# Hidden and gathered token operands interleaved in one tile, and every expert pass inside the two arms of TensorE's branch

## The chip, the cores and the metric

The kernel runs on one core of one Trainium2 chip. The metric is the device time of that core in microseconds, from launch to end, of the whole program. A core has TensorE for matrix products (PE in the profile, with its loads of the stationary operand listed apart as PEld), VectorE (DVE), ScalarE (ACT), GpSimd (POOL) and SyncE (SP), each with its own instruction queue, and 16 DMA engines. The on-chip memory SBUF has 128 partitions; matmul results go to the eight banks of PSUM.

## What is computed

The reference is a two-layer trunk over 256 tokens of width 1024: layer one is an RWKV-7 time mix and a dense SwiGLU block, layer two a forgetting attention and a mixture of experts, with an RMS norm ahead of each block and at the end. The change touches the mixture of experts:

```python
logits = (xf @ w_router).astype(jnp.float32)
top_v, top_i = lax.top_k(logits, K)            # K = 2 of E = 8 experts
gates = jax.nn.softmax(top_v, axis=-1)
...
def expert_block(args):
    e, tok, wt = args
    return swiglu(xf[tok], w_gu[e], w_down[e]).astype(jnp.float32) * wt[:, None]
```

`swiglu` is `(silu(x @ w_gate) * (x @ w_up)) @ w_down`, with inner width 3584. The 512 choices of 256 tokens spread over eight experts, 64 each on average. Everything is fp32.

## The kernel before, in words

**Precision.** TensorE multiplies in a one-pass fp32 format (`F32R`) that keeps fewer bits. Each operand is therefore split in two, a high part that is its cast (ACT) and a low part that is the rest (DVE): `split`, L213 to L215. A product is the sum of three passes: high weight by high token, low weight by high token, high weight by low token.

**Weights.** `Weights` (L166) streams all weights as tiles of 128x2048 fp32 (1 MB) from two DMA queues in turn, SP and POOL (L180). In the expert stage seven raw buffers are in use (three `wraw`, four `mob`; three more, `hpool`, take a tile once and later hold the hidden activations). Each tile is split to `wh` (four buffers) and `wl` (three buffers), two tiles ahead of their use in program order (`get`, L206). A raw buffer is free for the next DMA when its split is done; a `wh` or `wl` buffer when TensorE has used it.

**Order.** Up to the end of the RWKV block the order is written by hand. From there a scheduler orders the instructions of each engine by priority (their place in the program) and by when its own cost model has them ready, and places all semaphores. What stands inside a `tc.If` is one unit for it: nothing from outside is put between. Each engine then runs its list strictly in order.

**An expert** (`for e in range(E)`, L1639) has 42 weight tiles, 28 for gate and up and 14 for down, worked through in 21 pairs (`pair`, L1505). Gate and up go by chunks of the inner width, three of 1024 and one of 512 (`CH`, L373; `up_chunk`, L1541), down in seven pairs (`down`, L1587). The tokens are the stationary operand, 128 slots wide; the weights stream through, 512 columns per matmul.

**Short and long experts.** An expert with at most 64 tokens (short) leaves half the slots free, and these hold the low parts: slots 0 to 63 are the high parts, slots 64 to 127 the low parts of the same tokens. Two passes then give all three products, and a `fold` matmul (L1538, L1539) adds rows 64 to 127 to rows 0 to 63 of the result. ACT casts the result to `gc`, times a 0/1 factor `mode.short`, for it. The fold is issued for all experts; for one with more than 64 tokens (long) it adds zeros. Only the third pass, `third`, stands in a branch that TensorE alone takes (L1527), on the token count loaded into a register (L1641). A pair does `two(0)` for its first tile, `third` for both tiles in the branch, other work (`hooks[0]`), `two(1)`, `hooks[1]`.

**Around a chunk.** After gate's last pair comes `gc`, and in up's first pair the fold and SiLU (`first_half`). After up come `gc`, fold and product (`second_half`) in the next chunk's first pair, and in its second pair four TensorE transposes per 512 columns and their split into `hx` (`transposes`, L1562 to L1571): two ACT instructions for the two halves of the slots, a DVE subtraction, and a DVE multiply-add that puts the low parts of short experts into slots 64 to 127.

**Gather and scatter.** `gather` (L1463) takes the tokens of two experts at once: DVE builds one-hot matrices `ohs` from the slot positions, matmuls of 256 columns with the normed tokens `muh` and `mul` give `xgh` and `xgl` (48 matmuls in all), and ACT casts them. It also transposes the one-hots to `ohT` for `scatter` (L1596), which adds the gated result to `res`. The first gather stands before expert 0, the others in the down part of experts 1, 3 and 5. A fallback for experts with over 128 tokens (L1660) follows, and isn't entered with these inputs.

**Memory.** `mu32`, the normed tokens that the router reads (L1714), shares its place with `xgh`; `xgl` and `hx` have tiles of their own, `hx` with two high and two low parts one after the other.

## Time and profile before

| | |
|---|---|
| time, median of three runs | 1691.68 us (1690.11 to 1696.17) |
| time of the profiled execution | 1692.88 us |
| its span, first to last instruction | 1691.0 us |
| TensorE matmul busy | 1555.7 us (92%) |
| VectorE busy | 1297.7 us (77%) |
| ScalarE busy | 1106.7 us (65%) |
| DMA traffic | 445.73 MB, mean 264 GB/s |
| expert stage, first matmul to last | 713.1 to 1671.5 us |

The profile is of one execution. Busy times count work on the engine itself; waits, branches and the issue of DMAs aren't busy. In a row of a group, what is written stands left of the arrow and what is read right of it; then come the number of instructions, their busy time together, the mean duration of one in ns, and the engine's idle time just before them with what ended most of it. In a row of the timeline the first number is the start and the second the duration of a run of equal instructions. Matmuls are pipelined: four that take 1.07 us together start 0.23 us apart, though one alone shows 0.39.

### The profile page before, as it was taken

What the parts mean: (1) busy time and instruction counts of PE and PEld (TensorE: products, weight loads), DVE (VectorE), ACT (ScalarE), POOL (GpSimd) and SP (SyncE); (2) the same over time, 40 slices, a digit from 0 to 9 for tenths busy, and PEclk for the clock granted to TensorE, in tenths of its full rate; (3) what the DMA queues carried; (4) which work ended last, traced back from release to release, by engine and by line L of the source; (5) the groups of instructions that cost most, each with busy time, mean ns of one, the idle gap of its engine ahead of it and who ended that gap; (6) DMA issues with size and microseconds to landing.
All of it is one profiled execution on the core that took longest, in us unless ns stands there. A gap on an engine that the chain in (4) does not pass through costs nothing. (4 is left out here: it accounts for less than half of the span.)

```text
span 1691.0 us, 20004 instructions
## 1 busy us (share of the span) xinstructions
PE 1555.7 (92%) x7275; PEld 1201.5 (71%) x7275; DVE 1297.7 (77%) x1357; ACT 1106.7 (65%) x1148; POOL 176.7 (10%) x230
## 2 busy tenths in 40 slices
PE   5998998999999999998889999999988889888996
PEld 4655876888888887766566788788665567566885
DVE  5587557555546556699899888888899899998985
ACT  4633245444435665598688777677788798797783
POOL 0412010000000000011111111110111111111110
PEclk9998598999999999799899999999999999999999
DMA  5233133555555442579899999899899999999982
GB/s 178 88 109 104 22 106 132 189 180 199 183 193 181 150 150 100 224 297 384 347 397 370 364 357 362 327 358 341 312 387 397 360 401 370 382 383 368 373 338 84
DMA packets 156816, 445.73 MB, mean 264 GB/s; under 512 B 24129, under 2 KB 29425, under 8 KB 156705
## 3 DMA queue, kind: packets, MB, share of 16 engines
q1 hardware_dynamic: 105440, 262.95, 42.4%
q0 software_dynamic: 45920, 176.31, 27.5%
q10 hardware_dynamic: 5344, 5.01, 1.0%
q8 instruction: 67, 1.10, 0.3%
q14 instruction: 45, 0.36, 0.1%
HBM read 442.12 MB, written 2.11 MB: 263 GB/s over the span
## 5 line engine op out<-in xcount | busy, mean ns | idle before, releaser
L215 DVE TENSOR_TENSOR wl<-raw,wh 128x2048 fp32r<-128x2048 f32 x398 | 890.6, 2284 | 108.9 <-PE acc L219 35.3
L214 ACT CAST wh<-raw 128x2048 fp32r<-128x2048 f32 x398 | 752.6, 1914 | 304.4 <-PE pgu L220 51.4
L1503 PE MATMUL pgu<-wh,xgh 128*128 128x512 f32 x896 | 259.7, 408 | 10.5 <-ACT wh L214 3.9
L1503 PE MATMUL pgu<-wl,xgh 128*128 128x512 f32 x896 | 252.3, 403 | 13.7 <-DVE wl L215 13.7
L1503 PEld LDWEIGHTS pgu<-wh,xgh 128*128 128x128 f32 x896 | 169.5, 195 | 64.1 <-issue 22.5
L1503 PEld LDWEIGHTS pgu<-wl,xgh 128*128 128x128 f32 x896 | 171.7, 193 | 54.4 <-DVE wl L215 18.0
L1503 PE MATMUL acc<-wh,hx 128*128 128x512 f32 x616 | 165.2, 399 | 5.2
L180 POOL DMA_DIRECT2D raw<-in_moe_w_gu_dram x112 | 79.9, 714 | 668.7 <-DVE wl L215 556.4
L1503 PEld LDWEIGHTS acc<-wh,hx 128*128 128x128 f32 x616 | 113.3, 189 | 41.3 <-issue 12.7
L1503 PE MATMUL acc<-wl,hx 128*128 128x512 f32 x448 | 127.3, 402 | 3.0 <-DVE wl L215 2.1
L1503 PEld LDWEIGHTS acc<-wl,hx 128*128 128x128 f32 x448 | 82.2, 189 | 28.9 <-DVE wl L215 11.5
L218 PE MATMUL pgu<-wh,uh 128*128 128x512 f32 x224 | 89.3, 399 | 1.9 <-ACT wh L214 1.9
L219 PE MATMUL pgu<-wl,uh 128*128 128x512 f32 x224 | 88.2, 394 | 1.6 <-DVE wl L215 1.6
L220 PE MATMUL pgu<-wh,ul 128*128 128x512 f32 x224 | 88.2, 394 | 0.0
L1503 PE MATMUL pgu<-wh,xgl 128*128 128x512 f32 x336 | 85.0, 395 | 0.0
L1503 PE MATMUL pgu<-gc,fold 128*128 128x512 f32 x112 | 50.7, 464 | 37.1 <-ACT gc L1538 35.4
L1503 PEld LDWEIGHTS pgu<-wh,xgl 128*128 128x128 f32 x336 | 63.1, 188 | 14.9
L1538 ACT ACTIVATE gc<-pgu,cnt 128x512 fp32r<-128x512 f32 x112 | 72.3, 692 | 1.3 <-PE pgu L1503 1.3
L180 POOL DMA_DIRECT2D raw<-in_moe_w_down_dram x56 | 39.4, 704 | 294.8 <-DVE wl L215 165.2
L1503 PEld LDWEIGHTS pgu<-gc,fold 128*128 128x128 f32 x112 | 21.1, 189 | 64.0 <-ACT gc L1538 60.3
L1570 DVE TENSOR_TENSOR hx<-pht,hx 128x512 fp32r<-128x512 f32 x56 | 37.3, 689 | 32.2 <-ACT hx L1569 32.2
L219 PEld LDWEIGHTS pgu<-wl,uh 128*128 128x128 f32 x224 | 42.8, 191 | 10.7 <-DVE wl L215 2.0
(366 smaller groups left out, 2185.2 us busy)
## 6 DMA issues: line engine op xcount, KB each, us to landing
raw<-in_moe_w_gu_dram SPq DMA_DIRECT2D x112, 1024.0 KB, 9.6
raw<-in_moe_w_gu_dram POOLq DMA_DIRECT2D x112, 1024.0 KB, 9.7
raw<-in_moe_w_down_dram SPq DMA_DIRECT2D x56, 1024.0 KB, 8.9
raw<-in_moe_w_down_dram POOLq DMA_DIRECT2D x56, 1024.0 KB, 8.6
raw<-in_ffn_w_gu_dram SPq DMA_DIRECT2D x28, 1024.0 KB, 5.4
raw<-in_fox_w_in_dram SPq DMA_DIRECT2D x16, 1024.0 KB, 5.7
raw<-in_ffn_w_down_dram SPq DMA_DIRECT2D x14, 1024.0 KB, 4.9
raw<-in_rwkv_w_rkv_dram SPq DMA_DIRECT2D x24, 512.0 KB, 4.4
```

The source lines that it names most:

```text
L180: (nc.gpsimd if self.nd >= N_EARLY and self.nd % 2 else nc.sync).dma_start(t, src)
L214: nc.scalar.copy(hi, src)
L215: nc.vector.tensor_tensor(lo, src, hi.bitcast(F32), ALU.subtract)
L218: nc.tensor.matmul(o, lh, rh, start=first, stop=False)
L219: nc.tensor.matmul(o, lh, rl, start=False, stop=False)
L220: nc.tensor.matmul(o, ll, rh, start=False, stop=last)
L1503: nc.tensor.matmul(o, l, r, start=first, stop=last, skip_group_check=True)
L1538: nc.scalar.activation(gc, p, AF.Copy, scale=mode.short)
L1570: nc.vector.tensor_tensor(l, p, h.bitcast(F32), ALU.subtract)
```

## The change

- Both parts lie in turns in one tile: `xg` is `[128, KB, 2, 128, 2]` and `hx` `[128, 2, 4, 128, 2]`, the last index being high or low. A long expert reads 128 slots of one part with a step of two elements; a short one reads the first 64 slots of both parts, which lie next to each other, as 128. So nothing has to be placed into slots 64 to 127, and the hidden activations go by a plain `split`, written with a step of two.
- All passes of a pair stand in the branch: `passes(False)` in one arm (three passes per tile), `passes(True)` in the other (two). The fold and the transposes stand in the arms too (`arms`), after the pair's passes; the other work (`todo`) comes after the branch, once per pair.
- The fold is issued in the short arm alone; since high and low rows alternate, it adds odd rows to even ones. The cast to `gc` stays for all, without a factor. In the short arm the transposes are matmuls with `evens`, the identity with its even columns first.
- The gather makes the two parts by two products each; the one-hots for the scatter come from slot numbers (`slots`) halved for short experts by a new constant `half`.
- `mu32` moves to the tiles of `ul` in another pool, and `uh` and `ul` of the expert stage are made after the positions.

```diff
@@ fox
             if step == 12:
+                norm2.u32 = [npool.tile([128, 4, T], F32, name=f"mu32{i}", tag=f"ul{i}") for i in range(2)]
...
@@ gather
+            for i in range(n):
+                nc.vector.scalar_tensor_tensor(slots[:, i, :], cc("half"), shorts[i], cc("iota"), ALU.mult, ALU.add)
             for t in range(2):
-                nc.vector.tensor_scalar(oh2[:, t, 0:n, 0:64], cc("iota", 0, 64)[:, None, :].to_broadcast([128, n, 64]),
-                                        0.0, None, ALU.mult)
                 for i in range(n):
...
+                    nc.vector.tensor_scalar(ohs[:, 0, t, i, :], cc("iota"), pcols[i](t), None, ALU.is_equal)
+                    nc.vector.tensor_scalar(ohs[:, 1, t, i, :], slots[:, i, :], pcols[i](t), None, ALU.is_equal)
+            g = rot.tile([128, KB, 2, 128, 2], F32R, name="xg", bufs=1)
+            for part, src in enumerate((uh, ul)):
                 for k2 in range(4):
...
+                        for t in range(2):
                             nc.tensor.matmul(p[:, j * n * 128:(j + 1) * n * 128], src[t][:, k * 128:(k + 1) * 128],
-                                             o[:, t, 0:n, :], start=(q == 0), stop=(q == len(prods) - 1))
-                    nc.scalar.copy(g[:, k2 * 2:k2 * 2 + 2, 0:n, :],
+                                             ohs[:, 0, t, 0:n, :], start=(t == 0), stop=(t == 1))
+                    nc.scalar.copy(g[:, k2 * 2:k2 * 2 + 2, 0:n, :, part],
                                    p[:, 0:2 * n * 128].rearrange("p (j i t) -> p j i t", j=2, i=n))
...
@@ pair
-            def two(i):
...
-            def third():
...
+            def passes(short):
+                for i in range(2):
+                    for part, at in ((0, 0), (1, 0)) if short else ((0, 0), (0, 1), (1, 0)):
+                        for ti, j, k in blocks:
+                            if ti == i:
+                                l = lhs(k)[:, 0:64, :].rearrange("p s a -> p (s a)") if short else lhs(k)[:, :, at]
+                                for b, o in enumerate(out):
+                                    mm(o, l, ws[i][part][:, j, b * 512:(b + 1) * 512], k == 0 and part == at == 0,
+                                       i == 1 and part == 1)
+                for f in arms:
+                    f(short)
+
+            if many is None:
+                passes(False)
             else:
-                with tc.If(mode.many > 64):
-                    third()
...
+                with tc.If(many > 64) as arm:
+                    passes(False)
+                with arm.Else():
+                    passes(True)
+            for f in todo:
                 f()
...
@@ folded
-            nc.scalar.activation(gc, p, AF.Copy, scale=mode.short)
-            return lambda: mm(p, fold, gc, last=True)
+            nc.scalar.copy(gc, p)
+            return lambda short: short and mm(p, fold, gc, last=True)
...
@@ up_chunk
-            def transposes(b):
...
-                h, l = hidden(n0 // 512 + b)
-                nc.scalar.copy(h[:, :, 0:64], p[:, :, 0:64])
-                nc.scalar.activation(h[:, :, 64:128], p[:, :, 64:128], AF.Copy, scale=mode.other)
-                nc.vector.tensor_tensor(l, p, h.bitcast(F32), ALU.subtract)
-                nc.vector.scalar_tensor_tensor(h[:, :, 64:128], l[:, :, 0:64].bitcast(F32), mode.short,
-                                               h[:, :, 64:128].bitcast(F32), ALU.mult, ALU.add)
+            def transposes(is_short):
+                pht[:] = pht or [ps("pht") for _ in range(nb)]
+                for b in range(nb):
+                    for j in range(4):
+                        o, x = pht[b][:, j * 128:(j + 1) * 128], sgs[b][:, j * 128:(j + 1) * 128]
+                        if is_short:
+                            mm(o, x, evens, True, True)
+                        else:
+                            nc.tensor.transpose(o, x, ident)
+
+            def parts():
+                for b in range(nb):
+                    h = hidden(n0 // 512 + b)
+                    split(pht[b].rearrange("p (j t) -> p j t", j=4), h[:, :, :, 0], h[:, :, :, 1])
...
+                    pair(W, many, blocks, lambda k: g[:, k, i], p, arms.pop(0) if arms else [],
+                         ([first_half] if gu == 1 and q == 0 else []) + (todo.pop(0) if todo else []))
+                arms = [[folded(x, b) for b, x in enumerate(p)] + (arms.pop(0) if arms else [])]
+            return [[second_half], [parts]], [arms[0], [transposes]]
```

More of the change, by code (lines that the diff above doesn't have):

```diff
@@ L1411, in moe @@
         nc.vector.tensor_scalar(pos, pos, 1.0, None, ALU.subtract)
+        uh, ul = ([npool.tile([128, D], F32R, name=f"m{n}{t}", tag=f"{n}{t}") for t in range(2)] for n in ("uh", "ul"))
         for hf in range(2):
@@ L1438, in gates @@
             nc.vector.tensor_tensor(gate, gate, tm, ALU.add)
-        cnt = small([128, 2, E], "cnt")
         p = ps("pcn")
@@ L1454, in moe @@
-        nc.vector.tensor_scalar(fold[:, 64:128], ident[:, 64:128], 0.0, None, ALU.mult)
+        nc.vector.tensor_copy(fold[:, 0:127:2], ident[:, 1:128:2])
+        nc.vector.tensor_scalar(fold[:, 1:128:2], ident[:, 1:128:2], 0.0, None, ALU.mult)
+        evens = ident.rearrange("p (s a) -> p a s", a=2)
+        slots = pool.tile([128, 2, 128], F32, name="slots")
         prep.close()
-        class Mode:
-            def __init__(self, short, other, many=None):
-                self.short, self.other, self.many = short, other, many
@@ L1541, in up_chunk @@
-        def up_chunk(c, W, g, i, mode, todo):
+            nc.scalar.copy(gc, p)
+            return lambda short: short and mm(p, fold, gc, last=True)
+        def up_chunk(c, W, g, i, many, todo, arms):
             n0, w = CH[c]
             nb, a = w // 512, 2048 // w
-            todo = list(todo)
-            pgu, sgs, folds = [], [], []
+            todo, arms = list(todo), list(arms)
+            pgu, sgs, pht = [], [], []
             def first_half():
-                for b in range(nb):
-                    folds[b]()
@@ L1724, in tile_trunk @@
     else:
+        norm_moe.u32 = [fpool.tile([128, 4, T], F32, name=f"mu32{i}", tag=f"ul{i}") for i in range(2)]
         norm_moe.all()
```

112 lines of the change are left out of this document (32 added, 80 removed).

## The prediction

> **What bounds the kernel now.** I read the page's first two parts, then the expert stage cut into its eight experts, then who waits for whom in them. The profiled execution took 1692.9 us, 1.2 us above the median of the three timed runs (1691.7); the sums below start from 1692.9.
>
> ```profile
> 713.10:819.70 106.60, 96.52 (x387) 68.84 (x386) 100.61 (x62) 93.03 (x79) 13.50 (x19) 0.97 0.87 333
> 819.70:939.80 120.10, 104.94 (x436) 77.03 (x435) 110.59 (x84) 100.19 (x89) 14.80 (x21) 0.94 0.96 370
> 939.80:1067.30 127.50, 125.30 (x558) 102.00 (x557) 109.97 (x70) 97.59 (x81) 15.03 (x22) 1.00 0.93 361
> 1067.30:1199.70 132.40, 130.01 (x604) 107.03 (x604) 111.31 (x81) 100.73 (x89) 14.92 (x21) 1.00 0.89 334
> 1199.70:1312.40 112.70, 98.59 (x390) 70.17 (x390) 106.80 (x69) 93.52 (x79) 14.87 (x21) 0.97 0.97 373
> 1312.40:1431.00 118.60, 102.47 (x437) 75.56 (x436) 110.12 (x82) 100.60 (x89) 14.83 (x22) 0.97 0.97 375
> 1431.00:1542.90 111.90, 98.37 (x389) 69.32 (x388) 106.71 (x69) 94.50 (x79) 14.34 (x21) 0.97 1.00 387
> 1542.90:1671.50 128.60, 124.37 (x551) 100.55 (x550) 106.72 (x69) 91.59 (x78) 12.81 (x18) 1.00 0.80 308
> ```
>
> The columns are the stretch, its length, busy us of PE, PEld, DVE, ACT and POOL, granted clock, DMA share and GB/s. I cut at each expert's last `acc` matmul. Three experts (2, 3 and 7) have some 165 more matmuls (558 against 390): the third pass, 168 matmuls by the code, runs in them alone. I call them long, the five others short. A long expert is TensorE's: 125.3 of 127.5 us busy. In a short one VectorE is busy 106.8 of 112.7 us and the DMA nearly all the time, while TensorE has slack. So the same microsecond is worth different things in the two kinds.
>
> ```profile
> 1300.00:1320.00 20.00, 15.73 (x58) 11.04 (x57) 19.25 (x11) 14.49 (x10) 2.81 (x4) 0.94 1.03 411
> DVE res L1606 <- PE psc L1605: 11.5, 3, 6.0
> DVE hx L1570 <- ACT hx L1569: 7.0, 6, 2.1
> DVE wl L215 <- issue: 2.1, 2, 1.2
> ```
>
> The first row is the densest 20 us I found for the DMA, 411 GB/s. The others are all that VectorE waited for in experts 4 to 6 (343 us): 20.6 us, none of it for weights. So VectorE paces the short experts, with the DMA close behind.
>
> **The change, part by part.**
>
> *Branch.* Before, only the third pass stands in the branch.
>
> ```profile
> L1527 PEldq COMPARE_BRANCH  x231: 65/179/353, 712.9 to 1665.5; - x116
> L1527 PEldq EVENT_SEMAPHORE  x105: 51/51/51, 715.2 to 1540.3; - x105
>   ACT wh L214: 45.2, 41
> L1503 PE MATMUL pgu<-wl,xgh x896: 387/389/632, 714.1 to 1631.5; 128*128 128x512 f32 x180
> 726.44 0.87 PEld L1503 LDWEIGHTS pgu<-wl,xgh 128*128 128x128 f32 x4
> 727.85 0.53 PEld L1503 LDWEIGHTS pgu<-wh,xgh 128*128 128x128 f32 x3 [0.54 <-issue]
> 726.67 1.07 PE L1503 MATMUL pgu<-wl,xgh 128*128 128x512 f32 x4
> 727.88 0.93 PE L1503 MATMUL pgu<-wh,xgh 128*128 128x512 f32 x3
> ```
>
> There are 21 pairs of weight tiles per expert. 105 is 21 x 5: a semaphore instruction runs only where the pass is skipped, making up the signals of the skipped matmuls, and it waits for the matmuls before it. TensorE then stands: loads idle 0.54 us, the next matmul starts 0.30 us late (four matmuls take 1.07 and one 0.39 us, a step of 0.227; 726.67 + 4 x 0.227 = 727.58 against 727.88). 231 is 105 + 2 x 63: a long pair passes two branches and, in expert 2 with only 2.2 us without a matmul, loses nothing by them. ACT's casts waited 45.2 us in all for that semaphore instruction.
>
> After, each arm holds all passes. Both give the same signals (last use of each weight tile, last write), so in short experts the semaphore instruction should go: about 0.4 us (between 0.30 and 0.54) x 105 = 42 us of TensorE. This is worth nothing directly, since VectorE and DMA cover it. But the fold stands in the short arm alone, and each fold signals. In the eight pairs per long expert that carry folds (four gate, four up) the long arm must make up the difference: 24 x 0.4 = +9.6 us on the bound engine. Ends: 0 (nothing to make up) and 24 x 0.54 = 13. I take 9.6.
>
> *Folds.* Long experts lose 14 each.
>
> ```profile
> L1503 PE MATMUL pgu<-gc,fold 128*128 128x512 f32 x14 | 5.4, 409 | 1.1 <-ACT gc L1538 1.0
> L1503 PE MATMUL pgu<-gc,fold 128*128 128x512 f32 x14 | 6.9, 492 | 7.9 <-ACT gc L1538 7.6
> L1538 ACT ACTIVATE gc<-pgu,cnt 128x512 fp32r<-128x512 f32 x112 | 72.3, 692 | 1.3 <-PE pgu L1503 1.3
> L214 ACT CAST y<-acc 128x512 fp32r<-128x512 f32 x16 | 8.5, 584 | 9.6 <-PE acc L1503 9.6
> ```
>
> The first two rows are the fold in expert 2 and in expert 4. In long experts 3 x 14 x 0.227 = 9.5 us and about 1.0 us of waiting for `gc` go. In short ones the 7.9 us wait should go, for the fold now follows a whole pair (16 x 0.227 = 3.6 us) instead of half; again off the bound. ACT still casts `gc`, with a plain copy (`y` 584 ns against 692), off the bound.
>
> *Hidden activations.*
>
> ```profile
> L1570 DVE TENSOR_TENSOR hx<-pht,hx 128x512 fp32r<-128x512 f32 x56 | 37.3, 689 | 32.2 <-ACT hx L1569 32.2
> L1571 DVE SCALAR_TENSOR_TENSOR hx<-hx,cnt 128x256 fp32r<-128x256 f32 x56 | 24.7, 477 | 0.0
> L1569 ACT ACTIVATE hx<-pht,cnt 128x256 fp32r<-128x256 f32 x56 | 27.5, 492 | 0.0
> L1568 ACT CAST hx<-pht 128x256 fp32r<-128x256 f32 x56 | 20.8, 371 | 0.0
> raw<-in_moe_w_gu_dram SPq DMA_DIRECT2D x112, 1024.0 KB, 9.6
> raw<-in_moe_w_gu_dram POOLq DMA_DIRECT2D x112, 1024.0 KB, 9.7
> raw<-in_moe_w_down_dram SPq DMA_DIRECT2D x56, 1024.0 KB, 8.9
> raw<-in_moe_w_down_dram POOLq DMA_DIRECT2D x56, 1024.0 KB, 8.6
> ```
>
> L1571 goes: 7 x 0.44 = 3.1 us of VectorE per expert (24.7 us over eight). ACT's two become one of about 584 ns, 0.28 us less. L1570 stays, with steps of two elements. No row here shows such a step. Ends: 0 and a doubling (+4.7 us per expert, which would eat the gain); 0, after its own row. In five short experts that is 15.5 us of VectorE. The DMA allows less: 336 tiles of 1024 KB are 42 or 44.0 MB per expert, so three experts 3.1 us shorter each need 132/334 = 395 GB/s, against 387 where its share was 1.00 and 411 at best. I take 12; ends 0 and 26 (the DMA at 400 GB/s gives 110 us per expert, 440 against 463 in experts 1, 4, 5, 6, and 3 from expert 0). In long experts VectorE's gain is covered by TensorE.
>
> *Transposes and order.* In short arms a transpose becomes a plain fp32 matmul, perhaps twice as long:
>
> ```profile
> L1565 PE MATMUL pht<-C,sg 128*128 128x128 f32 x28 | 4.2, 272 | 0.0
> L1560 DVE TENSOR_TENSOR sg<-sg,pgu 128x512 f32<-128x512 f32 x7 | 4.5, 678 | 0.0
> L215 DVE TENSOR_TENSOR wl<-raw,wh 128x2048 fp32r<-128x2048 f32 x398 | 890.6, 2284 | 108.9 <-PE acc L219 35.3
> ```
>
> 28 x 0.27 = 7.6 us more at most, under the slack. They move to the arm's end. Behind them stands all of TensorE; they need `sg`, which VectorE multiplies (2 x 0.68) after the previous pair, 3.6 us earlier at least. At worst a 2.28 us weight split stands in front: 3.64, so the stall is near 0.
>
> *Gather.* It issues 32 of 48 matmuls, 10 VectorE instructions for 12.
>
> ```profile
> 1067.30:1199.70 132.40, 5.92 (x48) 5.89 (x48) 4.31 (x8) 1.00 0.89 334
> 708.81 0.41 PE L1485 MATMUL pgx<-ohs,muh 128*128 128x256 f32 x1
> 709.02 1.05 PE L1485 MATMUL pgx<-ohs,mul 128*128 128x256 f32 x4
> 713.11 1.17 PE L1503 MATMUL pgu<-wh,xgh 128*128 128x512 f32 x4
> ```
>
> One gather lies in a long expert (3): 16/48 x 5.9 = 2.0 us saved (that window row is of `pgx` alone). The first gather precedes all experts, at a slower step of (1.05 - 0.41)/3 = 0.21: 16 x 0.21 = 3.4 us, part of it behind VectorE's `mul`. I take 1.5; ends 0 and 3.4.
>
> *Stepped loads.* The long arm reads its stationary operand with a step of two: 3 x 504 = 1512 loads. Contiguous they take
>
> ```profile
> L1503 PEld LDWEIGHTS pgu<-wh,xgl 128*128 128x128 f32 x112 | 21.0, 188 | 5.0
> ```
>
> 188 ns, hidden under the 227 ns step with 39 to spare. No row has a stepped one. Ends: 188 and twice that. I take 188, the row of the same load and type.
> The Trainium skill, "SBUF — State Buffer", section "Door 1: The DMA port swizzle", says lines are 16 bytes and two hits per line keep full bandwidth; a step of two fp32 gives two, so by that rule the cost is nothing. No run here shows it.
>
> *Moved tiles.* `mu32` takes `ul`'s place, read last many microseconds before; `uh`/`ul` come after the router matmuls that read `mu32` and that the positions needed anyway. Nothing. The tile queues on SP and POOL issue the same 336 tiles.
>
> *Sum:* -1.5 (start) - 12 (short) + 9.6 - 9.5 - 1.0 - 2.0 (long) = -16.4: 1676.5 for the profiled execution, 1675 against the median.
>
> **Rivals.**
>
> *Both bounds give further* (0.15). No signals to make up, VectorE's 20.6 us of waits go too: -3.4 - 26 - 12.5 = -42, 1650. For it: ACT's 45 us behind the semaphore instruction. Against: the DMA has to hold 400 GB/s throughout.
>
> *The gain is swallowed* (0.17). In short experts the DMA share is 0.97 to 1.00 already, so VectorE's 12 is lost, and long experts trade folds for signals: about -4, 1688.
>
> *Slower: leaving the long arm isn't free* (0.10). Each long pair now jumps over the whole other arm and joins it. If TensorE drains there as on today's skip, 63 x 0.54 = +34. With -12.5 for folds and gather, -1.5, and half the short gain (-6): +14, 1706. It decides from (12.5 + 1.5 + 6)/63 = 0.32 us per pair. Against it: today's long pairs pass two branches without loss.
> The Trainium skill, "Runtime: NRT & Kernel Launch", section "Instruction fetch mechanics", speaks for it: a taken branch out of the prefetched window stalls for a fetch. By it such a jump would stall now and then; the row's longest branch, 353 ns against a median of 179, is small.
>
> *Slower: stepped loads* (0.08). At a quarter more, 235 + 39 = 274 against 227: 1512 x 0.047 = +71, 1746 after the gains. It decides from 16/1512, some 11 ns beyond the cover.
>
> **How the numbers follow.** The forecast (0.50) has its own range 1662 to 1685. A measurement tells about 0.5% (8.5 us) from no change. Faster is under 1683: 0.48 of the forecast and the first rival, 0.63. Same: 0.19. Slower: 0.18, the last two. The range reaches the first rival below and, since the slower cases hold 0.18, past the drain case above: 1650 to 1708.
>
> **What would show it.** Right: no semaphore instruction in short experts' pairs, 24 in long ones; 70 folds; short experts 2 to 4 us shorter with VectorE still near full; long ones within 3 us of today; loads 188 ns in long arms. Wrong: loads over 227 ns there, a gap after every long pair, or short experts unchanged at a DMA share of 1.00.

## The result, and the profile after

The changed kernel takes 1643.6 us (median of six runs, 1641.0 to 1656.8), the kernel before 1693.7 us beside it (1690.1 to 1697.8): a ratio of 0.971 with a 95% interval of 0.968 to 0.974. The forecast was 1675 in a range from 1650 to 1708, so the change gave three times as much as forecast, and the time lies below the range. The same kernel measured again, beside the later experiments, gave 1639.3 us and a ratio of 0.968 (0.965 to 0.971).

The first two lines are from the page of the changed kernel, busy times and instruction queue. The window view follows, cut at each expert's last `acc` matmul, with the columns that the prediction explains.

```profile
PE 1532.7 (93%) x7309; PEld 1203.6 (73%) x7309; DVE 1275.9 (78%) x1292; ACT 1089.5 (66%) x1092; POOL 176.4 (11%) x230
q8 instruction: 91, 1.49, 0.4%
```

```profile
701.10:801.10 100.00, 93.81 (x408) 70.62 (x409) 96.39 (x62) 90.14 (x73) 12.78 (x18) 1.00 0.92 354
801.10:917.30 116.20, 104.87 (x451) 79.09 (x451) 108.08 (x73) 100.39 (x83) 14.88 (x21) 0.96 1.01 392
917.30:1039.80 122.50, 122.50 (x541) 102.08 (x541) 109.11 (x64) 95.67 (x74) 15.59 (x22) 1.00 1.00 380
1039.80:1167.10 127.30, 127.13 (x578) 106.47 (x577) 108.52 (x73) 99.06 (x82) 14.89 (x21) 1.00 0.94 349
1167.10:1274.20 107.10, 97.91 (x416) 73.98 (x415) 102.46 (x62) 89.94 (x71) 14.20 (x20) 0.97 0.99 381
1274.20:1388.30 114.10, 103.84 (x451) 79.39 (x451) 106.76 (x71) 99.55 (x83) 14.88 (x21) 0.96 1.02 396
1388.30:1495.50 107.20, 98.36 (x415) 72.46 (x415) 104.86 (x63) 89.75 (x72) 14.88 (x21) 0.98 1.02 402
1495.50:1619.70 124.20, 122.89 (x540) 101.34 (x539) 105.35 (x62) 92.09 (x72) 12.78 (x18) 1.00 0.85 324
```

Each short expert (0, 1, 4, 5, 6) is 4 to 7 us shorter than before, each long one (2, 3, 7) 4 to 5. TensorE is now busy for all 122.50 us of expert 2; before, it stood 2.2 us there. In the short experts the DMA rate is up: 396 and 402 GB/s in experts 5 and 6, against 375 and 387. The span fell by 51.7 us:

| part of the span | before | after | change |
|---|---|---|---|
| RWKV block, up to its last five matmuls | 281.3 | 274.9 | -6.4 |
| from there to the first gather | 420.5 | 419.5 | -1.0 |
| first gather, to the first expert matmul | 11.3 | 6.7 | -4.6 |
| five short experts | 569.9 | 544.5 | -25.4 |
| three long experts | 388.5 | 374.1 | -14.4 |
| end | 19.4 | 19.5 | +0.1 |

The first row isn't the change's doing: that block's instructions and their order are the same in both kernels (the last section comes back to it). The comparisons below therefore go by the sums over the short and over the long experts. These repeat well: the second measurement of the changed kernel has 543.8 and 373.5, and no single short expert differs by more than 1.2 us.

Who waits in experts 4 to 6 now (the views of waits of VectorE and of ScalarE over the three experts, in us, times and the longest):

```profile
DVE wl L216 <- ACT wh L215: 11.9, 5, 3.1
DVE res L1590 <- PE psc L1589: 1.4, 2, 0.9
DVE wl L216 <- PE acc L1492: 1.2, 1, 1.2
DVE y L216 <- ACT y L215: 1.0, 1, 1.0
```

```profile
ACT wh L215 <- DMA raw<-in_moe_w_gu_dram: 22.3, 25, 2.8
ACT wh L215 <- PE pgu L1492: 8.0, 8, 2.8
ACT wh L215 <- DMA raw<-in_moe_w_down_dram: 5.9, 5, 1.4
ACT wh L215 <- PE acc L1492: 3.5, 3, 1.7
```

Before, 18.5 of VectorE's 20.6 us were for `psc` and `hx`; now most of its waits are for weights. ScalarE waits 28.2 us for transfers. Before it waited here 28.4 us behind the skipped pass's semaphore instruction and 16.6 for transfers:

```profile
ACT wh L214 <- PEq L1527: 28.4, 26, 3.4
ACT wh L214 <- DMA raw<-in_moe_w_gu_dram: 9.2, 13, 1.4
ACT wh L214 <- DMA raw<-in_moe_w_down_dram: 7.4, 9, 1.9
```

The changed kernel's instructions that the prediction named (views of the branch's line, of the matmul line and of the line of the long arm's transposes): 231 branches are left and no semaphore instruction at that line, and there are 70 folds. Each long expert has four semaphore instructions, 12 in all, at its transposes. In the short arm the 140 transposes have become 280 matmuls: each product by `evens` shows as two.

```profile
L1515 PEldq COMPARE_BRANCH  x231: 65/202/432, 700.6 to 1615.4; - x116
L1492 PE MATMUL pgu<-gc,fold x70: 387/495/796, 714.1 to 1469.2; 128*128 128x512 f32 x70
L1492 PE MATMUL pht<-C,sg x280: 273/274/278, 727.4 to 1473.9; 128*128 128x128 f32 x140
L1554 PEldq EVENT_SEMAPHORE  x12: 51/51/51, 971.8 to 1575.9; - x12
```

### The profile page after: what moved, and what is told of

Read it like the earlier page. It is cut to its first block, busy times and chain, and to the rows that moved or that the text cites. A ratio compares the mean times of both kernels' runs of the same rounds, so it can differ in the third digit from the quotient of the medians.

```text
span 1639.3 us, 19902 instructions
## 1 busy us (share of the span) xinstructions
PE 1532.7 (93%) x7309; PEld 1203.6 (73%) x7309; DVE 1275.9 (78%) x1292; ACT 1089.5 (66%) x1092; POOL 176.4 (11%) x230
## 5 line engine op out<-in xcount | busy, mean ns | idle before, releaser
L1492 PE MATMUL pgu<-wh,xg 128*128 128x512 f32 x1232 | 330.2, 401 | 2.0 <-issue 1.6
L1492 PEld LDWEIGHTS pgu<-wh,xg 128*128 128x128 f32 x1232 | 237.4, 195 | 53.1 <-issue 2.9
L1492 PE MATMUL pgu<-wl,xg 128*128 128x512 f32 x896 | 253.5, 405 | 12.9 <-DVE wl L216 10.0
L1492 PEld LDWEIGHTS pgu<-wl,xg 128*128 128x128 f32 x896 | 168.3, 193 | 70.7 <-DVE wl L216 37.4
L1525 ACT CAST gc<-pgu 128x512 fp32r<-128x512 f32 x112 | 61.1, 595 | 0.0
L1492 PE MATMUL pgu<-gc,fold 128*128 128x512 f32 x70 | 30.8, 479 | 21.9 <-ACT gc L1525 21.6
L219 PEld LDWEIGHTS pgu<-wh,uh 128*128 128x128 f32 x224 | 42.6, 190 | 10.6 <-ACT wh L215 2.1
L221 PEld LDWEIGHTS pgu<-wh,ul 128*128 128x128 f32 x224 | 42.6, 190 | 9.1
L219 PE MATMUL acc<-wh,hh 128*128 128x512 f32 x112 | 43.9, 392 | 0.0
L221 PE MATMUL acc<-wh,hl 128*128 128x512 f32 x112 | 43.7, 390 | 0.0
```

Source lines behind the costliest of these rows:

```text
L219: nc.tensor.matmul(o, lh, rh, start=first, stop=False)
L221: nc.tensor.matmul(o, ll, rh, start=False, stop=last)
L1492: nc.tensor.matmul(o, l, r, start=first, stop=last, skip_group_check=True)
L1525: nc.scalar.copy(gc, p)
```

## The experiments

### One part at a time

`arms_only` is the kernel before with the changed kernel's control flow (passes, folds and transposes in the arms) and the old layout, gather and VectorE work. ScalarE's cast to `gc` has no factor here either (604 against 690 ns in experts 4 to 6). Its `pair` is the changed one but for one line (against the changed kernel):

```diff
-                                l = lhs(k)[:, 0:64, :].rearrange("p s a -> p (s a)") if short else lhs(k)[:, :, at]
+                                l = lhs(k)[at]
```

> The branch alone: passes, fold and transposes stand in the arms as in the changed kernel, but the operands keep the old layout (separate high and low tiles, VectorE places the low parts of short experts, old gather, contiguous loads). Theory A (the semaphore instruction of the skipped pass paced short experts, through ScalarE's casts that waited 45.2 us behind it): most of the 25 us gained in short experts comes with this alone, and long experts gain as in the changed kernel or 2 to 3 us more each, for their loads take 188 ns and not 193: 1645 to 1655. Theory B (VectorE's work paced short experts, and the 128x256 multiply-add of 0.44 us that went is what gave the time): short experts stay within 1 us of the 107 to 120 us they had, only long ones gain: 1672 to 1680.

Measured: 1654.7 us, ratio 0.978 (0.974 to 0.982). Short experts 557.4 us (-12.5), long ones 369.1 (-19.4; the changed kernel has 374.1). The arms alone give half of the short experts' gain and more than all of the long ones'. The short experts one by one, in us, with two kernels that come further down:

| expert | before | `arms_only` | changed | `mid_fold_skip` | `all_back` |
|---|---|---|---|---|---|
| 0 | 106.6 | 104.1 | 100.0 | 105.1 | 106.1 |
| 1 | 120.1 | 118.5 | 116.2 | 115.6 | 119.6 |
| 4 | 112.7 | 107.1 | 107.1 | 111.0 | 108.7 |
| 5 | 118.6 | 119.3 | 114.1 | 113.5 | 116.0 |
| 6 | 111.9 | 108.4 | 107.2 | 111.3 | 107.6 |

In experts 4 and 6 the arms give nearly the whole gain. What they don't give lies in expert 0 and in experts 1 and 5, in whose down part a gather stands.

`skip_back` is the changed kernel with a branch after each pair that a short expert skips, and so with 105 drains of TensorE again:

```diff
                 with arm.Else():
                     passes(True)
+                with tc.If(many > 64):
+                    mm(out[0][0:64, 0:8], fold[:, 1:128:2], ws[0][0][:, 0, 0:8])
```

> The changed kernel with a skipped branch put back behind each pair: one tiny matmul that adds zeros, taken by long experts alone, so that short ones again run a semaphore instruction that waits for TensorE to drain (105 in all). Theory A: short experts lose 3 to 5 us each, and long ones some 0.1 us per pair: 1643.6 + 15 to 25 + 6, about 1665 to 1675. Theory B: TensorE has slack in short experts, so only the 6 us: about 1650.

Measured: 1658.6 us, 0.979 (0.975 to 0.983). TensorE waits for its sequencer as much as it should (first row: experts 4 to 6 together; then TensorE's waits in them), but these three experts take 328.6 us, as in the changed kernel (328.4):

```profile
1183.00:1511.60 328.60, 292.12 (x1280) 221.31 (x1278) 314.82 (x194) 282.65 (x225) 43.96 (x62) 0.99 1.01 395
```

```profile
PE pgu L1492 <- PEq L1519: 20.5, 37, 0.9
PE acc L1492 <- PEq L1519: 8.5, 17, 0.6
```

All short experts together are 3.7 us longer, and expert 0 alone is 4.1; the long ones are 6.0 us longer, 0.1 us for each of the 63 small matmuls. So in experts 4 to 6 29 us of drains alone fit into TensorE's slack. These drains are longer than those of the kernel before:

```profile
1192.08 1.07 PE L1492 MATMUL pgu<-wl,xg 128*128 128x512 f32 x4
1193.70 1.17 PE L1492 MATMUL pgu<-wh,xg 128*128 128x512 f32 x4 [0.56 <-PEq L1519]
```

Here the next matmul starts 0.71 us late (1192.08 + 4 x 0.227 = 1192.99), where the prediction found 0.30 before. In experts 4 to 6 the median from the last matmul ahead of a skip to the first behind it is 0.86 us, against 0.55 before and a step of 0.23 without a skip.

`dve_back` is the changed kernel with a VectorE instruction of the size of L1571 put back for each 512 columns:

```diff
                     split(pht[b].rearrange("p (j t) -> p j t", j=4), h[:, :, :, 0], h[:, :, :, 1])
+                    nc.vector.scalar_tensor_tensor(slots.rearrange("p a (b c) -> p (a b) c", c=64),
+                                                   h[:, :, 0:64, 1].bitcast(F32), cc("iota", 0, 1),
+                                                   h[:, :, 64:128, 0].bitcast(F32), ALU.mult, ALU.add)
```

> The changed kernel with the 128x256 VectorE multiply-add put back as idle work (its result goes to a spare place): 56 instructions of about 0.48 us, 3.1 us of VectorE per expert. Theory B: short experts lose it all, 5 x 3.1 = 15.5 us: about 1659. Theory A, with the DMA now the bound of short experts (share 1.01 and 402 GB/s in expert 6): under 1 us per expert, 1644 to 1648.

Measured: 1644.1 us, 0.972 (0.967 to 0.976); short experts 541.5 us, not longer than without it. The kernel before and `dve_back`, experts 4 to 6:

```profile
1199.70:1542.90 343.20, 299.44 (x1213) 215.05 (x1212) 323.64 (x218) 288.61 (x246) 44.04 (x62) 0.97 0.98 378
```

```profile
1168.60:1495.30 326.70, 297.99 (x1280) 220.50 (x1279) 323.82 (x217) 280.74 (x225) 43.96 (x62) 0.99 1.02 399
```

VectorE does the same 323.6 to 323.8 us of work in both, in one case within 343.2 us and in the other within 326.7. Its work didn't set the pace. One side effect is in the sum: in `dve_back` the four one-hots for the scatter come behind all those for the gather, not in turns with them, and experts 1 and 5, which hold these gathers, are 4.2 and 2.2 us shorter than in the changed kernel. But in experts 4 and 6, without a gather, the difference is -0.8 and +1.2 us, where 3.1 us of work were added to each.

`gather_48` gives the changed kernel's gather 48 matmuls again; `gather_back` does so too and adds the two VectorE additions that have to wait for the last of them:

```diff
-                        for t in range(2):
+                        for t in (0, 1, 0, 1) if part == 0 else (0, 1):
...
+            for t in range(2):
+                nc.vector.tensor_tensor(ohs[:, 0, t, 0:n, 64:128], ohs[:, 0, t, 0:n, 64:128].bitcast(F32),
+                                        ohs[:, 1, t, 0:n, 64:128].bitcast(F32), ALU.add)
```

> The changed kernel with the 16 matmuls of each gather that the change removed issued again (the high product is made twice, the second time from scratch). If the shorter gather is what brought the first expert matmul 4.7 us nearer to the first gather matmul, and 2 us in expert 3: +5 to +6, about 1649. If the order of VectorE's and ScalarE's work did it: +2 or less.

> This is the changed kernel with the old gather's cost put back: 48 matmuls instead of 32, and two VectorE additions on the one-hots that have to wait for the last of these matmuls, as L1491 did before. Theory K (the gather is the other half of the short experts' gain): experts 1 and 5, in whose down part a gather lies, get 3 to 6 us longer each than 116.2 and 114.1, the five short experts together go to 550 to 557 us. Rival L (the loads are hidden one by one, and only their sum shows): 542 to 549 us.

Measured: 1651.2 us, 0.974 (0.970 to 0.978), and 1649.4, 0.972 (0.967 to 0.978). Both have 546.5 us in the short experts (+2.0) and 1.3 us more in expert 3. In experts 1 and 5 `gather_back` costs 1.5 and 2.4 us, and expert 4 is 2.6 us shorter. The gather isn't the other half of the short experts' gain. Nor did fewer matmuls shorten the first gather: with 48 it took 8.2 us, as with 32 (6.7 and 8.5).

`fold_both` issues the fold in the long arm too, with zero columns:

```diff
-            return lambda short: short and mm(p, fold, gc, last=True)
+            return lambda short: mm(p, fold, gc, last=True) if short else mm(p[0:64, :], fold[:, 1:128:2], gc, last=True)
```

> This is the changed kernel with the fold issued in the long arm too, there with zero columns. If the removed folds were worth their place in TensorE's stream, the three long experts get 42 x 0.233 = 9.8 us longer (374.1 to about 384 us), plus about 1 us of waiting for gc, and the whole goes to about 1654 us. Rival (the folds were hidden, and the long experts' gain of 14.4 us came from gaps that closed): long experts stay within 3 us of 374 us. Short experts are unchanged under both.

Measured: 1648.9 us, 0.976 (0.970 to 0.982). Long experts 382.6 us, 8.5 to 9.1 more than in the two measurements of the changed kernel; short ones 543.6. Expert 2 has 14 matmuls more and takes 125.70 instead of 122.50 us, 0.229 us for each:

```profile
920.30:1046.00 125.70, 125.70 (x555) 104.06 (x555) 109.02 (x64) 95.28 (x74) 15.59 (x22) 1.00 0.99 371
```

### The stepped loads

`twice` puts the parts side by side again, 128 low slots and then 128 high ones. In a short expert the gather writes each token into slots s and s + 64, so the 128 slots in the middle are its low and its high parts; long and short reads are both contiguous, and one set of one-hots serves gather and scatter.

```diff
-                                l = lhs(k)[:, 0:64, :].rearrange("p s a -> p (s a)") if short else lhs(k)[:, :, at]
+                                l = lhs(k).rearrange("p a s -> p (a s)")[:, 64:192] if short else lhs(k)[:, 1 - at]
...
-                            mm(o, x, evens, True, True)
+                            mm(o, x, twice, True, True)
```

> This is the changed kernel with the two parts side by side again: 128 low slots, then 128 high slots. In a short expert the gather puts each token into slots s and s + 64, so that the 128 slots in the middle are the low and the high parts and every stationary operand is contiguous. Theory (the step of two on the long experts' stationary loads costs 5.6 ns on each of 1512 matmuls, 0.233 against 0.2275 us): loads are 188 ns again, the three long experts together are some 8 us shorter than the changed kernel's 374.1 us (365 to 368), the short ones unchanged (540 to 547), about 1635 us in all. Rival (the wider spacing comes from the arms being longer, not from the step): long experts stay at 372 to 376 us and the whole at 1641 to 1647 us.

> The contiguous version (twice) again, beside the changed kernel on the same chip. Stepped loads cost 4 to 6 ns on 1512 matmuls: the three long experts 5 to 8 us shorter than in the run of the changed kernel beside it, the whole 4 to 10 us faster. If the first run of it was scatter: within 3 us.

> The changed kernel again, for the comparison beside it: 1641 to 1648 us, long experts 372 to 375 us together.

Measured: 1637.0 us, 0.966 (0.960 to 0.972), and measured again 1637.6, 0.966 (0.963 to 0.970), beside 1639.3 for the changed kernel. Long experts 367.5 and 364.8 us against 374.1 and 373.5. The loads of expert 2, the changed kernel's and then those of `twice`, and below them `twice`'s window of that expert (groups by line and shape: count, busy us, mean ns, idle before):

```profile
L1492 PEld LDWEIGHTS pgu<-wh,xg 128*128 128x128 f32 x225 | 43.6, 194 | 8.6
L1492 PEld LDWEIGHTS acc<-wh,hx 128*128 128x128 f32 x112 | 21.6, 194 | 4.2
```

```profile
L1491 PEld LDWEIGHTS pgu<-wh,xg 128*128 128x128 f32 x224 | 41.9, 188 | 8.6
L1491 PEld LDWEIGHTS acc<-wh,hx 128*128 128x128 f32 x112 | 20.9, 188 | 4.4
```

```profile
927.60:1047.40 119.80, 119.77 (x541) 98.94 (x540) 109.06 (x64) 95.17 (x74) 15.58 (x22) 1.00 1.01 387
```

The same 541 matmuls take 119.80 instead of 122.50 us: 2.7 us over 504 stepped loads, 5.4 ns each. The step lengthens a load by about the same 6 ns, though even the longer load, 194 ns, is 33 ns shorter than the 227 ns step of the matmuls. The median step of the 512-column matmuls in expert 2 is 233 ns in the changed kernel and 227 in `twice`. Little of it reached the whole time. `twice`'s expert stage is 909.2 and 906.1 us against 918.6 and 917.3, but its first gather began at 707.3 and 707.2 us against 694.4 and 691.0. Six of these 13 to 16 us TensorE stood ahead of the gather, until VectorE was past the one-hots, which there depend on the token counts. `twice_early` makes the counts right after the router's ranks:

> This is twice with the token counts, and the factor for short experts that comes from them, made right after the router's ranks, ahead of the positions. In twice the one-hots of the gather hang on that factor, and TensorE stood 6.2 us ahead of the first gather. If that stand is what ate the gain of the contiguous operands, it falls below 2 us, and the whole goes from 1637 to 1630 to 1634 us, with the expert stage at 905 to 910 us. Rival (something else in the start is late then, as the low parts of the tokens): the first gather starts no earlier, 1635 to 1639 us.

Measured: 1643.2 us, 0.969 (0.967 to 0.971), a miss. The stand ahead of the gather fell from 6.2 to 2.5 us, not below 2, and the gather itself grew from 6.4 to 8.7 us, since it now waits for the tokens' own parts; the expert stage has 911.2 us, and the RWKV block, which is the same, ended 5.6 us later than in `twice`. `twice` is the fastest of the complete kernels tried, but against the changed kernel beside it its lead (1.6 us of medians) is within the scatter.

### What set the pace of the short experts

Since neither VectorE's work nor the drains alone explain the gain, the next runs changed the order of things. `before_late` is the kernel before, with the split of the hidden activations and the additions to `res` later:

```diff
-            return [[second_half], []] + [[lambda b=b: transposes(b)] for b in range(nb)]
+            turn = [lambda b=b: transposes(b) for b in range(nb)]
+            late = [lambda b=b: parts(b) for b in range(nb)]
+            return [[second_half], [], turn] + ([[late[0]], late[1:]] if c == 3 else [late] if c == 2 else [[], late])
```

> This is the kernel before with only the order of other work changed: VectorE's and ScalarE's split of the hidden activations stands one to two half pairs later, behind two more weight splits, and the scatter's additions to res stand one and two pairs behind its split of y. No branch, layout or instruction count changes. Theory C (in short experts VectorE lost time by standing in order behind TensorE's psc and ScalarE's hx, 20.6 us of waits in experts 4 to 6): these waits fall below 8 us and the five short experts together come down from 569.9 us by 12 to 25 us, towards the changed kernel's 544.5. Rival D (the order is not what matters; the gain needs the skipped pass's semaphore instruction gone, behind which ScalarE waited 45.2 us): short experts stay at 563 to 572 us. Under both the long experts stay at 383 to 390 us.

Measured: 1700.0 us, 1.004 (1.000 to 1.007); short experts 570.7 us, long ones 400.5, which is 12.0 us more than before and outside what either theory gave. VectorE's waits for `psc` in experts 4 to 6 went from 11.5 to 0.3 us, but others came in their place, 17.8 us in all:

```profile
DVE wl L215 <- issue: 6.7, 7, 2.3
DVE wl L215 <- ACT hx L1571: 5.2, 6, 1.4
DVE hx L1573 <- ACT hx L1572: 3.6, 3, 1.2
DVE wl L215 <- ACT wh L214: 1.6, 3, 0.9
```

`before_early` moves the kernel before's branch up by eight matmuls, so that `wh` comes free earlier; `late_release` exchanges the two passes of a short expert in the changed kernel, so that it comes free later:

```diff
-            two(0)
+            two(0, (0,))
             if mode.many is None:
...
                     third()
+            two(0, (1,))
```

```diff
-                    for part, at in ((0, 0), (1, 0)) if short else ((0, 0), (0, 1), (1, 0)):
+                    turn = ((1, 0), (0, 0)) if short else ((0, 0), (0, 1), (1, 0))
+                    for part, at in turn:
...
```

> This is the kernel before with its branch moved up by eight matmuls: a pair does the high-weight half of its first tile, then the branch with the third pass, then the low-weight half of that tile, and the rest as before. The skipped pass's semaphore instruction, by which a short expert's wh buffer comes free, then runs 1.8 us (8 x 0.227) earlier. Layout, number of drains, folds and VectorE's work stay. Theory E (before, ScalarE's casts were held by the late release of wh, 28.4 us of waits in experts 4 to 6, and so raw buffers came free late and the DMA ran at 373 to 387 GB/s): ScalarE's waits behind that instruction fall below 10 us in experts 4 to 6, those for the DMA rise, and the five short experts together come down from 569.9 us by 10 to 25 us. Rival F (the time of release doesn't matter; the gain needs the fold and the transposes at the end of the pair, or the plain order of the arms): 564 to 573 us, with waits of ScalarE moved to another cause.

> This is the changed kernel with the two passes of a short expert's tile exchanged: low weights first, then high weights, so a wh buffer comes free after the tile's last matmul instead of after its first half, 4 to 8 matmuls (0.9 to 1.8 us) later, and a wl buffer that much earlier. Long experts are as in the changed kernel. Theory E: ScalarE's casts wait for TensorE again (above 15 us in experts 4 to 6 against 11.5), and the five short experts together get 5 to 20 us longer than 544.5. Rival F: 541 to 548 us.

Measured: 1700.1 us, 1.005 (1.001 to 1.009), and 1668.9, 0.988 (0.983 to 0.993). In `before_early` ScalarE's waits behind the semaphore instruction fell from 28.4 to 5.5 us in experts 4 to 6, yet short experts went to 574.0: an earlier release alone didn't bring the gain. In `late_release` short experts are 14.6 us longer, as theory E gave, but there TensorE waits 33.7 us for `wl`, which it now needs first and which VectorE makes last, and the long experts, whose passes didn't change, are 13.8 us longer as well. The profiled execution took 1684.7 us, 16 more than the median, so both sums are high. It tells nothing of the release.

Left was TensorE's own chain (theory H). `mid_fold` puts the fold back into the middle of a short pair, `mid_fold_skip` adds `skip_back`'s drains, and `before_fold_late` delays fold, SiLU and product in the kernel before by half a pair:

```diff
-                for f in arms:
-                    f(short)
+                    for f in arms:
+                        if (f.__name__ == "transposes") == (i == 1):
+                            f(short)
```

```diff
-                        hooks[0] = [first_half] + hooks[0]
+                        hooks[1] = [first_half] + hooks[1]
...
-            return [[second_half], []] + [[lambda b=b: transposes(b)] for b in range(nb)]
+            return [[], [second_half], [], [lambda b=b: transposes(b) for b in range(nb)]]
```

> This is the changed kernel with the fold moved from the end of a short pair to its middle, between the passes of its two tiles, where it stood before the change; no drains. Theory H (before, TensorE's own chain set the pace of short experts, by waits for gc ahead of the fold and by drains at the skipped pass together; either alone fits into its slack): TensorE's waits for gc rise in experts 4 to 6 from 14 to about 25 us, and the five short experts stay within 6 us of 544.5. Rival (the fold's place alone was the gain): short experts go up by 12 to 25 us.

> This is mid_fold with the 105 skipped branches and their drains put back after each short pair as well (in long experts a matmul of 64x8 runs in each). Theory H: TensorE's waits for gc and for its sequencer together exceed its slack, so the five short experts go up by 12 to 25 us over 544.5, to 557 to 570, with ScalarE waiting for TensorE more than for the DMA. Rival (the two are hidden together as well, so something else set the pace): within 8 us of 544.5.

> This is the kernel before with the folds, SiLU and product one half pair later, at the end of the next pair, and the transposes at the end of the pair after it; drains, layout, branches and VectorE's work stay. Theory H: TensorE's waits for gc in experts 4 to 6 fall from 24.5 us to under 12, drains alone fit into the slack, and the five short experts together come down from 569.9 us by 8 to 20 us. Rival (the place of the fold does nothing for them): 565 to 574 us.

Measured: 1646.1 us, 0.975 (0.970 to 0.979); 1661.4, 0.982 (0.977 to 0.986); 1691.1, 0.999 (0.996 to 1.002). `mid_fold`: waits for `gc` up from 14.3 to 22.2 us, short experts 545.1, so hidden. `mid_fold_skip`: 556.5, 12.0 more than the changed kernel, where the two parts alone cost 0.6 and 3.7. In experts 4 to 6 alone it is 7.4 us more (335.8 against 328.4), where each part by itself has 328.6. These experts, and TensorE's waits there:

```profile
1177.20:1513.00 335.80, 295.11 (x1280) 224.62 (x1278) 317.22 (x195) 283.43 (x226) 44.77 (x63) 0.98 1.00 390
```

```profile
PE pgu L1492 <- PEq L1520: 18.1, 33, 0.7
PE pgu L1492 <- ACT gc L1528: 7.9, 3, 2.8
PE acc L1492 <- PEq L1520: 7.2, 14, 0.6
```

So the two parts cost more together than alone. But TensorE's waits don't explain it as theory H has it: its waits for `gc` are 7.9 us, less than in `mid_fold` (22.2) and in the changed kernel (14.3), and those for its sequencer 25.3, less than in `skip_back` (29.0). What grew with both is ScalarE's wait for TensorE to free `wh`, 34.7 us against 13.3 (`mid_fold`) and 28.7 (`skip_back`), and VectorE's for ScalarE's casts, 17.6 against 7.8 and 12.0.

`before_fold_late` speaks against theory H, which gave 8 to 20 us less: it has 569.7 us, as the kernel before had, though its waits for `gc` fell to 16.4 us only, not below 12. And that `arms_only`, which takes drains and mid-pair folds out of the kernel before, gave 12.5 us, about what they cost here, isn't a proof that they were these 12.5: the drains here are longer, and `arms_only` also takes out the cut of each pair and the factor of `gc`.

`all_back` then puts most of it back into the arms: `mid_fold_skip`, `dve_back` and `gather_back` together.

> This is the changed kernel with all of it put back in its arms: the mid-pair fold, the 105 drains after short pairs, VectorE's multiply-add of each 512 columns and the old gather's matmuls and additions. Layout and stepped operands stay. Theory L (each engine of the ring DMA, ScalarE, VectorE, TensorE is near full, so that each load alone is hidden and only their sum shows): short experts at 562 to 572 us, near the kernel before's 569.9, against 556.5 with the fold and the drains alone. Theory K alone: 556.5 plus what gather_back adds. Rival (neither; something that isn't put back here, as the cut of the pair into two units by the branch): under 559 us.

Measured: 1667.9 us, 0.983 (0.979 to 0.988). Short experts 558.0 us, 1.5 more than `mid_fold_skip` and 11.9 short of the kernel before. Experts 4 to 6, and VectorE's waits in them:

```profile
1188.80:1521.00 332.20, 293.69 (x1296) 222.23 (x1294) 323.78 (x219) 282.50 (x225) 43.95 (x62) 1.00 1.01 394
```

```profile
DVE ohs L1483 <- PE pgx L1478: 4.4, 1, 4.4
DVE wl L216 <- ACT wh L215: 3.7, 5, 1.9
```

VectorE has the kernel before's work (323.78 against 323.64 us), TensorE has the drains, and the stretch is still 11.0 us shorter; VectorE's waits are 12.5 us less (8.1 against 20.6). By experts (the table under `arms_only`), 0 and 1 are back within 0.5 us of the kernel before, and 4, 5 and 6 are 4.0, 2.6 and 4.3 us short of it. In experts 4 and 6 the parts cost less here than in `mid_fold_skip`, though more work was added: they don't add up, and what drains and folds cost depends on the order around them.

Two things aren't put back. One is the cut of each pair into two units by a branch in its middle, with other work in between. The other is ScalarE's work: 282.50 us against 288.61, since `gc` has no factor (22.9 against 27.0 us in these experts) and `hx` is cast by one instruction instead of two (12.5 against 17.9). The scheduler also orders VectorE's and ScalarE's instructions a little differently in several of these kernels. A branch in the middle of a pair can't be put back without undoing the arms, and moving the work about in the kernel before (`before_late`, `before_fold_late`) didn't shorten its short experts. So the second half of the short experts' gain is narrowed down to the cut, ScalarE's 6.1 us and the order, and none of them is shown to be its cause.

`half_dma` asks what bounds the short experts now. It transfers half of each expert weight tile and splits that half into both halves of the tile, so half of the weights are left out and the result is another one:

```diff
+                elif w == 1024:
+                    q.dma_start(t[:, :, 0:512], src[:, :, 0:512])
+                else:
+                    q.dma_start(t[:, 0:2], src[:, 0:2])
```

> This is the changed kernel with only half of each expert weight tile transferred; both halves of the tile are then split from that half, so the products are of other weights, and the work of TensorE, VectorE and ScalarE is as large as before. Theory (after the change the short experts are bound by the DMA, at 392 to 402 GB/s): the short experts fall from 544.5 us to what VectorE or TensorE needs, 98 to 104 us each, some 510 us together; long experts change by under 3 us. Rival (VectorE, still busy 92 to 98% there, or the order of its work sets the pace): short experts stay within 6 us of 544 us.

Measured, in a single run: 1624.7 us; short experts 526.4, long ones 372.2. Experts 4 to 6:

```profile
1164.20:1481.30 317.10, 292.74 (x1280) 218.85 (x1279) 313.42 (x194) 284.19 (x226) 44.07 (x62) 1.00 0.67 207
```

The transfers do bound the short experts now, but only by 3%: without them VectorE is busy 313.42 of 317.10 us, so its work is the next bound there.

## Why the prediction was wrong

Its sum of -16.4 us met -51.7 in the profile, 6.4 of these in a block that wasn't touched. By its terms the first rival came nearest (-3.4, -26 and -12.5 against -4.6, -25.4 and -14.4), though partly by luck: in its long experts two things that it left out, longer loads and waits for `wl`, cancel.

**Short experts, -12 against -25.4: the main miss.** The step that failed is "VectorE paces the short experts, with the DMA close behind", and with it the costing of the gain by L1571's work. `dve_back` gives that work back at no cost. What the runs showed in its place: the control flow alone, with all of VectorE's work kept, gives 12.5 us (`arms_only`). The sentence that a drain "is worth nothing directly, since VectorE and DMA cover it" was right for the drains alone (at most 3.7 us, `skip_back`), but drains and mid-pair folds together cost 12.0 (`mid_fold_skip`). Shares of 94% (VectorE, 323.64 of 343.20 us) and 98% (DMA) side by side hid this. VectorE's 20.6 us of waits, which the prediction quoted, said that it didn't run at its own pace; the prediction read from them only that it didn't wait for weights. Which of its waits went by which part of the change stays open, and so does the cause of the other 12.9 us, as told above. The first rival took these waits away and let the DMA set the bound at 400 GB/s; the rates are 381 to 402 in experts 1, 4, 5 and 6 now.

**Signals in the long arm, +9.6 against 0.** The step "the long arm must make up the difference" failed. No semaphore instruction stands at the branch's line any more; the long arm has 4 per expert at its transposes, where 8 were forecast at the folds, and TensorE has no idle time in expert 2. Of the bounds that were given, the lower one, 0, was it.

**Folds in the long experts, -9.5: right.** `fold_both` measures 8.5 to 9.1 us, 0.229 us each in expert 2, against 0.227.

**Waits in the long experts, -1.0: too small.** The prediction counted the wait for `gc` alone. TensorE also waited for `wl` in the kernel before (experts 2, 3 and 7):

```profile
PE pgu L1503 <- DVE wl L215: 1.1, 1, 1.1
PE pgu L1503 <- DVE wl L215: 2.3, 1, 2.3
PE pgu L1503 <- DVE wl L215: 2.8, 2, 2.3
```

With 1.0 us for `gc` and 1.4 for `y` these are 8.6 us, and in `arms_only` 0.4 us of waits are left in the long experts. With the folds' 9.5 that makes most of its 19.4. None of these waits was for a branch; the sentence that a long pair "loses nothing" by its two branches holds.

**Stepped loads, 0 against +8.** The prediction took a load of 188 ns with 39 ns to spare. Measured: 194 ns, and the cost isn't hidden, 5.4 ns for each load in expert 2, which is 8 us over 1512 (`twice`: long experts 7 to 9 us shorter). So the cover of 39 ns was wrong. The prediction's own rival priced a longer load as load plus 39, and 194 + 39 is the 233 ns that the matmuls take. The Trainium skill, "SBUF — State Buffer", section "Door 1: The DMA port swizzle", counts 16-byte lines and lets two hits per line keep full bandwidth; by that the step of two fp32 would be free. For this load the trace differs, by 3% of the load. The rival's quarter more per load didn't come.

**Gather, -2.0 and -1.5 at the start.** In expert 3 it is 1.3 us (`gather_48`, `gather_back`). The first gather became 4.6 us shorter in the first profile and 2.8 in the second (11.3 to 6.7 and 8.5), around the upper end of 3.4, but not by its fewer matmuls (`gather_48`: 8.2).

**Leaving the long arm** cost nothing: 122.50 us busy of 122.50 in expert 2. The rival in which TensorE drains there fell, though more code is fetched (91 packets against 67 before, in the instruction queue's row):

```profile
q8 instruction: 67, 1.10, 0.3%
```

The Trainium skill, "Runtime: NRT & Kernel Launch", section "Instruction fetch mechanics", says that a taken branch out of the fetched window stalls. The longest branch here took 432 ns against 353 before, and no such stall shows in the long experts.

**Transposes, nothing: right in the sum.** The "perhaps twice as long" came about: each product shows as two matmuls of 274 ns, where a transpose was one of 272, and in expert 4 the 56 of them take 6.0 us of TensorE's stream against 2.5 for 28. What this costs the short experts wasn't measured by itself; they are shorter all the same.

**Steps in VectorE's and ScalarE's writes.** VectorE's 689 ns for `hx` stayed 689, as the prediction took it. ScalarE's cast takes 624 ns, not 584.

The long experts in sum: -2.9 forecast, -14.4 measured. The signals that weren't needed are 9.6 us of the difference and the waits 6 (8.6 before, 1.5 left in the changed kernel, where 1.0 less was forecast); the stepped loads took 8 back. Some 4 to 5 us are not assigned.

## What to carry to other kernels

Where several engines are each over 85% busy in one ring of buffers, price an edit by what each engine waits for in its fixed order, not by the work of the busiest one; and put parts back one by one and then together, since stalls that are hidden alone can cost much in sum, and can cost less again beside other work. Two whole alternatives in the arms of a branch can be cheaper than a skipped piece in the middle: 105 drains went, and nothing came for them in the longer arm.

## What the runs showed of the hardware

The RWKV block, the same instructions in the same order in every kernel here, ended anywhere from 268.7 to 281.3 us. Its windows (from the start, up to its last five matmuls) in the kernel before, the changed kernel and `fold_both`:

```profile
0.00:281.30 281.30, 249.06 (x1471) 179.63 (x1472) 184.58 (x391) 111.06 (x198) 49.88 (x53) 0.89 0.34 102
```

```profile
0.00:274.90 274.90, 242.02 (x1471) 172.67 (x1471) 184.79 (x391) 110.85 (x198) 49.85 (x53) 0.92 0.36 104
```

```profile
0.00:268.70 268.70, 233.94 (x1471) 166.82 (x1471) 185.22 (x391) 110.88 (x198) 49.81 (x53) 0.95 0.36 107
```

The granted clock of TensorE differs, 0.89, 0.92 and 0.95, over the same 1471 matmuls; VectorE's busy time doesn't. The kernel before and its three reordered forms all ended this block at 279.5 to 281.3 us, the other kernels between 268.7 and 281.0. Why isn't known from these runs. It means that some 6 us of the profiled difference, and perhaps as much of the timed one, come from stages that weren't touched, and that a change in one stage is better judged by that stage's own length.

A step of two on the stationary operand costs 5 to 6 ns per load (194 against 188 ns), and this reaches the matmul although the load is 33 ns shorter than the matmul's step of 227 ns. And with ScalarE at 85%, TensorE at 91%, VectorE at 96% and the DMA's share at 1.01 (experts 4 to 6 of the changed kernel), two stalls that cost 0.2 us each alone cost 7.4 together there (`mid_fold`, `skip_back`, `mid_fold_skip`), and 3.8 with further work added (`all_back`).
